# Opening of a two-layer backbone kernel: the first row sums of squares by TensorE, tile by tile, and the first projections by tiles of features

## The chip, the cores and the metric

The kernel runs on one core of one Trainium2 chip, as one program. The metric is the device time of one execution in microseconds (us). Three plain runs of the kernel before took 1098.90, 1098.99 and 1103.02 us, so the time before is their median, 1098.99 us. One more execution was recorded by the hardware profiler; every row below is from that one.

## The reference, cut to what matters

All tensors are float32. There are 1024 latent tokens and 256 context tokens of 1024 features, and two layers. Only the start of layer 0 matters here:

```python
def rms_norm(x, g):
    y = x * lax.rsqrt(jnp.mean(x * x, axis=-1, keepdims=True) + EPS)
    return y * g
def modulate(x, g, shift, scale):
    return rms_norm(x, g) * (1.0 + scale) + shift

shift, scale, gate = split(silu(c) @ ada_w[0] + ada_b[0], 3)
h  = modulate(x, norm_g[0], shift, scale)         # latent tokens
hc = modulate(ctx, norm_g[0], shift_c, scale_c)   # context tokens
kc, vc = split_kv(hc @ w_in[:, K0:G0], k_g)
q, k, v = split_qkv(h @ w_in, q_g, k_g)
...
```

After that come differential attention over 1280 keys, a Fourier mixer, a gated output projection, and a second layer with a short convolution.

## The kernel before, in words

x lies transposed: a tile of x holds 128 features (its partitions) by 512 tokens. There are eight feature tiles (k = 0 to 7) for each half of the tokens, `xs[0]` and `xs[1]`, and eight tiles of 128 features by 256 tokens for the context, `xc`.

The sum of squares of a token therefore runs over the partitions of eight tiles. Before, ScalarE squares each of the eight tiles (lines 196 and 199), VectorE adds the squares up elementwise into two running tiles `ssq` and then adds these two (lines 200 and 202), and TensorE sums over partitions at the end (`token_sums`, line 209): for each block of 128 tokens a product of the 128x128 block of `ssq` as the stationary operand with one column of ones, whose result is one column of `ps_ss`. Four blocks of tokens make four such products for a half of the latents, two for the context.

From `ps_ss` the rows of 1/rms are made by a chain through four engines: VectorE (216), GpSimd's power (218), a diagonal matrix `dg` by VectorE (220), a product of ones with it by TensorE (228, `ps_r`), a copy by ScalarE (234, `r`). Then `x_scale` (387) multiplies a tile of x by its scale and by `r`, `x_hi` (393) adds the shift and rounds to float32r, and `x_lo` (397) keeps the rest. Scale and shift of a feature tile come from `ada_first` (123), `ada_ev` (128), `ada_col` (135) and `ada_use` (144, 147, 150). For the first half, tile k = 0 has its scales from the first call of `ada_first`, k = 1 from the second.

A projection is computed for tiles of 128 tokens by 512 outputs. Six of them, `accs[0]` to `accs[5]`, are open at once in PSUM: four tiles of latents of the first half and then two of context. `proj_step` adds the share of one feature tile to one of them by three products (284 to 286: hi by hi, lo by hi, hi by lo). `steps(j, i...)` does that for the feature tiles 2j and 2j + 1, for each of the named accumulators in turn.

The order on TensorE, VectorE, ScalarE and GpSimd in the opening is that in which the code is written (`manual_schedule`); DMAs are issued by SyncE. An engine works off its queue in order, so an instruction that waits holds back all behind it. The buffers named `sq` come from a pool slot of four, which `ada_ev` shares.

Of the kernel before, what the change touches and what calls it, by code (L numbers as in the profile page):

```python
# [8 lines left out]
F32 = mybir.dt.float32  # L9
F32R = mybir.dt.float32r  # L10
AF = mybir.ActivationFunctionType
# [6 lines left out]
P = 128  # L18
# [4 lines left out]
KT = 8  # L23
# [6 lines left out]
NB = 512  # L30
# [7 lines left out]
def block_kernel(tc, A):  # L38
    nc = tc.nc
# [3 lines left out]
    def opn(name, side="left", space=None):  # L43
        kw = dict(name=name, bufs=1, side=side, reuse_waits="tile")
        if space is not None:
            kw["space"] = space
        cm = tc.tile_pool(**kw)
        pools[name] = (cm, cm.__enter__())
        return pools[name][1]
# [19 lines left out]
    pst = opn("pst", space=PSUM)  # L69
# [9 lines left out]
    ones = const.tile([P, P], F32, name="ones")  # L79
# [6 lines left out]
    xs = [[None] * KT for _ in range(2)]  # L86

    def load_x(half):
# [9 lines left out]
        out=cs[:, :, 0:2], in_=small[:, S_C:S_C + 16].rearrange("p (k r) -> p k r", r=2), func=AF.Silu)  # L98
# [5 lines left out]
        out=bias1, in0=small[:, S_B:S_B + 48].rearrange("p (l k) -> p l k", l=2)[:, :, 8:16],  # L104
# [84 lines left out]
    def squares_sum(tiles, n, pool):  # L189

        a = [pool.tile([P, NB], F32, name="ssq", tag="th", bufs=2) for _ in range(2)]

        def step(k):
            dst = a[k % 2]
            if k < 2:
                nc.scalar.activation(out=dst[:, :n], in_=tiles[k], func=AF.Square)
            else:
                sq = pool.tile([P, NB], F32, name="sq", tag="o", bufs=4)
                nc.scalar.activation(out=sq[:, :n], in_=tiles[k], func=AF.Square)
                nc.vector.tensor_add(out=dst[:, :n], in0=dst[:, :n], in1=sq[:, :n])  # L200
            if k == KT - 1:
                nc.vector.tensor_add(out=a[0][:, :n], in0=a[0][:, :n], in1=a[1][:, :n])
        return step, a[0]

    def token_sums(parts, n):
        ps = pst.tile([P, 8], F32, name="ps_ss", tag="t", bufs=2)
        for i in range(n // P):
            for a in parts:
                nc.tensor.matmul(ps[:, i:i + 1], lhsT=a[:, i * P:(i + 1) * P], rhs=ones[:, 0:1],
                                 start=a is parts[0], stop=a is parts[-1])  # L210
        return ps
# [40 lines left out]
    post = opn("post", "right")  # L252
# [24 lines left out]
    def proj_step(ps, tt, c, k):  # L277
        if tt < NTC:
            hh, hl = (a[:, tt * P:(tt + 1) * P] for a in HC[k])
        else:  # L280
            half, o = divmod(tt - NTC, 4)
            hh, hl = (a[:, o * P:(o + 1) * P] for a in H[half][k])
        whi, wlo = (w[:, (k % 2) * NB:(k % 2 + 1) * NB] for w in W[4 * c + k // 2])
        nc.tensor.matmul(ps, lhsT=hh, rhs=whi, start=k == 0, stop=False)  # L284
        nc.tensor.matmul(ps, lhsT=hl, rhs=whi, start=False, stop=False)  # L285
        nc.tensor.matmul(ps, lhsT=hh, rhs=wlo, start=False, stop=k == KT - 1)  # L286
# [8 lines left out]
    def proj_tok(tt, c, at=()):  # L295
        ps = acc.tile([P, NB], F32, name="ps_tok", tag="acc", bufs=6)
        for k in range(KT):
            if k in at:
                tick()
            if k == 7:  # L300
                tick(cols)
            proj_step(ps, tt, c, k)
        return ps
# [70 lines left out]
    for k in range(KT):  # L374
        t = hcp.tile([P, TC], F32, name="xc", tag="hc", bufs=17)
        nc.sync.dma_start(out=t, in_=A["ctxT"][k])
        xc.append(t)
    first = [2, 3, 4, 5, 0, 1]
    accs = [acc.tile([P, NB], F32, name="ps_tok", tag="acc", bufs=6) for _ in first]
# [41 lines left out]
    def steps(j, *tiles):  # L421
        for i in tiles:
            for k in (2 * j, 2 * j + 1):
                proj_step(accs[i], first[i], 0, k)

    def diag(ps, n):
        return rms_diag(ps, n, post, ("sqk", 1))

    def ada_ps():
        return pst.tile([P, NB], F32, name="ps_ada", tag="t", bufs=2)  # L430
# [12 lines left out]
        gt[w] = (t1, t2)  # L443

    HA, HB = slice(0, NB), slice(NB, 2 * NB)
    sq0, a0 = squares_sum(xs[0], NB, post)
    for k in range(KT):
        sq0(k)
    ps = token_sums([a0], NB)
    psa = ada_ps()  # L450
    ada_first(psa, araw[0])
    d0 = diag(ps, NB)
# [23 lines left out]
    def ada_next():  # L476
        psa = ada_ps()
        a = araw.pop(0)
        ada_half(psa, a, 0)
        ada_half(psa, a, 1)  # L480
        return ada_ev(psa)
# [3 lines left out]
        whalf(raw, w, HA, G)  # L485
        whalf(raw, w, HB, G)

    steps(0, 0, 1)
    psc = token_sums([ac], TC)
    dc = diag(psc, TC)  # L490
    steps(0, 2)
    ev = ada_next()
    w_split()
    araw.append(ada_load(0, 3))
# [104 lines left out]
    for tt in range(NK):  # L599
# [5 lines left out]
        ps = proj_tok(tt, 1, (4,))  # L605
        if tt:
# [4 lines left out]
                          in_=v.rearrange("p (h d) -> p h d", h=NH))  # L611
# [504 lines left out]
    def proj_feat2(w, half, at={}):  # L1116
        ps = acc.tile([P, NB], F32, name="ps_feat", tag="acc", bufs=6)
        for k in range(KT):
            if k in at:
                at[k]()  # L1120
            a, b = (w[k // 4][:, i, (k % 4) * P:(k % 4 + 1) * P] for i in range(2))
            nc.tensor.matmul(ps, lhsT=a, rhs=Y[half][k][0], start=k == 0, stop=False)  # L1122
            nc.tensor.matmul(ps, lhsT=a, rhs=Y[half][k][1], start=False, stop=False)
            nc.tensor.matmul(ps, lhsT=b, rhs=Y[half][k][0], start=False, stop=k == KT - 1)
        return ps
# [304 lines left out]
    for half in range(2):  # L1430
        y0(half)
        for f in range(KT):
# [5 lines left out]
            if pend:  # L1438
                ps = pend.pop(0)
            else:  # L1440
                ps = proj_feat2(W[half * KT + f], half)
# [229 lines left out]
```

## Time and profile before

| what | value |
|---|---|
| runs of the kernel | 1098.90, 1098.99, 1103.02 us |
| profiled execution, its own time | 1103.36 us |
| its span (first to last instruction) | 1101.6 us |
| mean granted TensorE clock | 0.981 |
| TensorE busy | 1037.6 us, 94% of the span |
| VectorE, ScalarE, GpSimd busy | 69%, 44%, 44% |
| DMA traffic | 131.12 MB, mean 119 GB/s |

Times in the rows are microseconds from the start of the span. PE is TensorE's matmuls and PEld its weight loads; a float32 product is recorded as two passes, so four products stand as x8. A row of the timeline gives start, duration, engine, line, operation, output<-inputs, shapes and count, and behind it in brackets the idle time ahead of it with what ended it. A row of the table by stretches gives, for a stretch of the span, its length, the busy time and number of instructions of PE, PEld, DVE, ACT and POOL, then the granted TensorE clock (1.00 is full, 0.50 half), the DMA share and GB/s. Ahead of the first record of the clock, which falls at about 21.9 us, the column reads 1.00 by default.

### The profile page before, as it was taken

Reading aid. Unit: us, or ns where it says so; the run is one execution under the profiler, and the core shown is the slowest. Engines: PE = TensorE matmul, PEld = TensorE weight load, DVE = VectorE, ACT = ScalarE, POOL = GpSimd, SP = SyncE. Lnnn points to the kernel's source line nnn. Section 1 sums busy time; section 2 is a strip of 40 time slices with the busy share of each in tenths; the row PEclk is TensorE's granted clock in tenths of the full one; section 3 lists DMA queues with packets and bytes.
Section 4 is the critical chain, followed back from the end, with each engine's and each line's share of the span. In section 5 each row is a group of like instructions: output and inputs, shape, how many; then the busy total and the mean of one; then the engine's idle time right before and its main releaser. Section 6 shows DMA issues by size and latency. Waiting matters only on the chain.

```text
span 1101.6 us, 14113 instructions
## 1 busy us (share of the span) xinstructions
PE 1037.6 (94%) x5118; PEld 846.6 (77%) x5118; DVE 756.2 (69%) x1079; ACT 481.7 (44%) x876; POOL 484.6 (44%) x412
## 2 busy tenths in 40 slices
PE   3998999999999899999999998899999999999798
PEld 2666888878877689899888886578888888787576
DVE  4599966957886388888853287985636645579842
ACT  4353323312445377777753363633333333353420
POOL 1247115620455047766574445655354353432331
PEclk9999999999999999999999998999999999999899
DMA  9733896353112978161006560121111112212421
GB/s 330 302 124 94 247 378 226 106 153 129 58 43 77 247 178 188 31 167 58 11 21 207 170 194 22 38 77 39 60 55 58 58 39 69 66 57 67 159 95 62
DMA packets 61381, 131.12 MB, mean 119 GB/s; under 512 B 5248, under 2 KB 30208, under 8 KB 58112
## 3 DMA queue, kind: packets, MB, share of 16 engines
q1 hardware_dynamic: 60240, 125.64, 35.9%
q0 software_dynamic: 1072, 4.59, 1.2%
q8 instruction: 40, 0.66, 0.2%
q14 instruction: 29, 0.24, 0.1%
HBM read 105.57 MB, written 24.64 MB: 118 GB/s over the span
## 4 chain that ended last, share of the span: by engine, by line
PE 64%; DVE 20%; POOL 5%; issue 5%; ACT 5%; DMA 0%; ACTq 0%; POOLq 0%; DVEq 0%
PE psX L651 6%; PE psX L653 6%; PE psX L652 6%; PE ps_av L1069 5%; PE ps_tok L284 3%; PE ps_tok L285 3%; PE ps_tok L286 3%; PE psY L652 3%; PE psY L653 3%; PE psY L651 3%; PE S L1019 3%; PE S L1020 3%; DVE nm L1024 2%; PE ps_t L1059 2%; PE ps_feat L1122 2%
## 5 line engine op out<-in xcount | busy, mean ns | idle before, releaser
L61 ACT CAST wop<-wraw 128x512 fp32r<-128x512 f32 x152 | 93.1, 620 | 127.4 <-PE psY L653 30.1
L62 POOL TENSOR_TENSOR wop<-wraw,wop 128x512 fp32r<-128x512 f32 x72 | 100.8, 1403 | 70.4 <-ACT wop L61 68.8
L284 PE MATMUL ps_tok<-whi,hhi 128*128 128x512 f32 x288 | 118.6, 412 | 4.5 <-ACT hhi L393 3.6
L285 PE MATMUL ps_tok<-whi,hlo 128*128 128x512 f32 x288 | 115.2, 400 | 3.8 <-DVE hlo L397 3.8
L286 PE MATMUL ps_tok<-wlo,hhi 128*128 128x512 f32 x288 | 114.3, 397 | 0.0
L1024 DVE TENSOR_REDUCE nm<-S 128x1 f32<-128x1280 f32 x64 | 95.1, 1487 | 22.4 <-PE S L1020 19.4
L651 PE MATMUL psX<-B,wop 128*128 128x512 f32 x240 | 98.2, 409 | 12.0 <-DVE out L1400 3.9
L1035 ACT ACTIVATE p<-S,nm 128x1280 f32<-128x1280 f32 x64 | 85.2, 1331 | 45.0 <-DVE nm L1024 41.2
L652 PE MATMUL psX<-B,wop 128*128 128x512 f32 x240 | 97.4, 406 | 1.6 <-POOL B L1491 1.0
L653 PE MATMUL psX<-B,wop 128*128 128x512 f32 x240 | 97.0, 404 | 0.5 <-POOL wop L62 0.5
L630 POOL TENSOR_TENSOR s<-wraw 128x512 f32<-128x512 f32 x20 | 27.6, 1382 | 125.1 <-DMA wraw<-in_wodd_dram 118.1
L62 DVE TENSOR_TENSOR wop<-wraw,wop 128x512 fp32r<-128x512 f32 x80 | 66.5, 833 | 20.6 <-ACT wop L61 20.3
L1069 PE MATMUL ps_av<-v,aT 128*128 128x128 f32 x640 | 76.8, 275 | 0.0
L630 POOL TENSOR_TENSOR wraw<-wraw 128x512 f32<-128x512 f32 x40 | 56.5, 1420 | 43.2 <-DVE wop L62 35.8
L1069 PEld LDWEIGHTS ps_av<-v,aT 128*128 128x128 f32 x640 | 74.2, 192 | 0.2
L284 PEld LDWEIGHTS ps_tok<-whi,hhi 128*128 128x128 f32 x288 | 55.3, 192 | 18.6 <-ACT hhi L393 4.5
L1046 POOL TENSOR_TENSOR p<-p,cc 128x256 f32<-128x256 f32 x32 | 40.3, 1258 | 65.7 <-DVE cc L1043 46.5
L285 PEld LDWEIGHTS ps_tok<-whi,hlo 128*128 128x128 f32 x288 | 55.2, 192 | 17.9 <-DVE hlo L397 7.1
L651 PEld LDWEIGHTS psX<-B,wop 128*128 128x128 f32 x240 | 46.3, 193 | 27.0 <-issue 5.4
L652 PE MATMUL psY<-B,wop 128*128 128x512 f32 x160 | 63.5, 397 | 2.7 <-DVE B L1253 2.3
L653 PE MATMUL psY<-B,wop 128*128 128x512 f32 x160 | 63.3, 396 | 1.5 <-DVE wop L62 1.5
L286 PEld LDWEIGHTS ps_tok<-wlo,hhi 128*128 128x128 f32 x288 | 55.2, 192 | 12.0 <-DVE wlo L172 0.2
(339 smaller groups left out, 2661.8 us busy)
## 6 DMA issues: line engine op xcount, KB each, us to landing
ada_raw<-in_ada_dram SPq DMA_DIRECT2D x24, 1024.0 KB, 8.0
wraw<-in_wodd_dram SPq DMA_DIRECT2D x32, 512.0 KB, 3.5
wraw<-in_wo_dram SPq DMA_DIRECT2D x24, 512.0 KB, 4.3
wraw<-in_wtok_dram SPq DMA_DIRECT2D x16, 512.0 KB, 5.8
arena<-kd SPq DMA_DIRECT2D x16, 320.0 KB, 8.9
kq<-kd SPq DMA_DIRECT2D x16, 320.0 KB, 9.6
xt<-in_xT_dram SPq DMA_DIRECT2D x16, 256.0 KB, 6.4
xr<-in_xT_dram SPq DMA_DIRECT2D x16, 256.0 KB, 3.9
```

The source lines that it names most:

```text
L61: nc.scalar.copy(out=o[:, 0, :], in_=src)
L62: eng.tensor_tensor(out=o[:, 1, :], in0=src, in1=f32(o[:, 0, :]), op=ALU.subtract)
L284: nc.tensor.matmul(ps, lhsT=hh, rhs=whi, start=k == 0, stop=False)
L285: nc.tensor.matmul(ps, lhsT=hl, rhs=whi, start=False, stop=False)
L286: nc.tensor.matmul(ps, lhsT=hh, rhs=wlo, start=False, stop=k == KT - 1)
L630: tt = lambda out, x, y, op: nc.gpsimd.tensor_tensor(out=out, in0=x, in1=y, op=op)
L651: nc.tensor.matmul(ps, lhsT=a, rhs=x[k][0], start=start and k == 0, stop=False, skip_group_check=not start)
L652: nc.tensor.matmul(ps, lhsT=a, rhs=x[k][1], start=False, stop=False, skip_group_check=not start)
L653: nc.tensor.matmul(ps, lhsT=b, rhs=x[k][0], start=False, stop=k == 3, skip_group_check=not start)
L1024: nc.vector.tensor_reduce(out=nm, in_=S[m][:, :NKEY], op=ALU.max, axis=AX.X, negate=True)
L1035: nc.scalar.activation(out=p, in_=S[m][:, :NKEY], func=AF.Exp, bias=tiles.pop((i, m, "nm")), accum_out=z)
L1069: nc.tensor.matmul(ps, lhsT=groups[i, k // 4][:, (k % 4) * P:(k % 4 + 1) * P], rhs=v[:, k * P:(k + 1) * P], start=k == 0, stop=k == NK - 1)
```

## The change

The squares of the first half of the latents are no longer added up by VectorE. ScalarE squares a feature tile, and TensorE at once sums its four blocks of tokens over partitions and adds the result to `ps_ss` in PSUM: four products for each of eight tiles, in place of four in all. The second half and the context keep the old way. Further down, the first six steps on TensorE are written out with the feature tile as the outer loop (accumulators 0, 1, 2 for k = 0, and then for k = 1), and the sums of the context's squares, which stood between accumulators 1 and 2, stand behind all of them.

```diff
-    sq0, a0 = squares_sum(xs[0], NB, post)
+    ps = pst.tile([P, 8], F32, name="ps_ss", tag="t", bufs=2)
     for k in range(KT):
-        sq0(k)
-    ps = token_sums([a0], NB)
+        sq = post.tile([P, NB], F32, name="sq", tag="o", bufs=4)
+        nc.scalar.activation(out=sq, in_=xs[0][k], func=AF.Square)
+        for i in range(4):
+            nc.tensor.matmul(ps[:, i:i + 1], lhsT=sq[:, i * P:(i + 1) * P], rhs=ones[:, 0:1], start=k + i == 0,
+                             stop=k == KT - 1, skip_group_check=i > 0)
     psa = ada_ps()
     ada_first(psa, araw[0])
     d0 = diag(ps, NB)
...
-    steps(0, 0, 1)
+    for k in range(2):
+        for i in range(3):
+            proj_step(accs[i], first[i], 0, k)
     psc = token_sums([ac], TC)
     dc = diag(psc, TC)
-    steps(0, 2)
     ev = ada_next()
```

On TensorE, the start of the queue (- before, + after; the names are output<-inputs, x4 and x32 count products):

```order
-L1664 UNCONDITIONAL_BRANCH
-L209 MATMUL ps_ss<-ones,ssq 128x1 x4
+L1670 UNCONDITIONAL_BRANCH
+L453 MATMUL ps_ss<-ones,sq 128x1 x32
 L123 MATMUL ps_ada<-ada_raw,cs 32x256 x8
 L228 MATMUL ps_r<-dg,ones 128x512
```

Thirty-two products now stand ahead of `ada_first` and `ps_r`, where four stood.

On TensorE, the first steps of the projections, before (ps_tok_152, 153 and 154 are accumulators 0, 1 and 2; hhi_219 and hlo_220 are the feature tile k = 0, hhi_243 and hlo_244 are k = 1):

```order
L284 MATMUL ps_tok_152<-whi_202,hhi_219 128x512
L285 MATMUL ps_tok_152<-whi_202,hlo_220 128x512
L286 MATMUL ps_tok_152<-wlo_203,hhi_219 128x512
L284 MATMUL ps_tok_152<-whi_202,hhi_243 128x512
L285 MATMUL ps_tok_152<-whi_202,hlo_244 128x512
L286 MATMUL ps_tok_152<-wlo_203,hhi_243 128x512
L284 MATMUL ps_tok_153<-whi_202,hhi_219 128x512
L285 MATMUL ps_tok_153<-whi_202,hlo_220 128x512
L286 MATMUL ps_tok_153<-wlo_203,hhi_219 128x512
```

and after (152, 153 and 154 are the same accumulators; hhi_240 is k = 0, hhi_264 is k = 1):

```order
L284 MATMUL ps_tok_152<-whi_223,hhi_240 128x512
L285 MATMUL ps_tok_152<-whi_223,hlo_241 128x512
L286 MATMUL ps_tok_152<-wlo_224,hhi_240 128x512
L284 MATMUL ps_tok_153<-whi_223,hhi_240 128x512
L285 MATMUL ps_tok_153<-whi_223,hlo_241 128x512
L286 MATMUL ps_tok_153<-wlo_224,hhi_240 128x512
L284 MATMUL ps_tok_154<-whi_223,hhi_240 128x512
L285 MATMUL ps_tok_154<-whi_223,hlo_241 128x512
L286 MATMUL ps_tok_154<-wlo_224,hhi_240 128x512
L284 MATMUL ps_tok_152<-whi_223,hhi_264 128x512
```

Before, three products stand ahead of the first that needs k = 1; after, nine. The context's two sums (line 209, `ps_ss`) come behind twelve products before and behind eighteen after; in both, the next conditioning products (line 117) come behind all eighteen.

On VectorE the seven adds leave the queue:

```order
 L271 COPY gains<-small 128x64
 L265 TENSOR_SCALAR g_102<-small 128x1
-L200 TENSOR_TENSOR ssq<-ssq,sq 128x512 x6
-L202 TENSOR_TENSOR ssq<-ssq 128x512
 L216 TENSOR_SCALAR rs<-ps_ss 128x4
 L220 TENSOR_TENSOR dg<-cst,rs 128x512
```

ScalarE has eight squares of the same size in both. Behind the steps shown, and on GpSimd and SyncE from the first row on, the queues read the same.

## The prediction

> **What bounds the kernel.** I read the page first, then the opening in order of time, then its busy times by stretches, then the same kind of work wherever it occurs later.
>
> ```profile
> span 1101.6 us, 14113 instructions
> ...
> PE 1037.6 (94%) x5118; PEld 846.6 (77%) x5118; DVE 756.2 (69%) x1079; ACT 481.7 (44%) x876; POOL 484.6 (44%) x412
> ```
>
> TensorE is busy for 94% of the span, so a time gained or lost in the opening is gained or lost whole unless something later takes it up. The opening in order of time:
>
> ```profile
> 5.95 0.63 ACT L196 ACTIVATE ssq<-xt 128x512 f32<-128x512 f32 x1 [0.92 <-DMA xt<-in_xT_dram]
> 7.46 0.63 ACT L196 ACTIVATE ssq<-xt 128x512 f32<-128x512 f32 x1 [0.89 <-DMA xt<-in_xT_dram]
> 8.13 2.60 ACT L199 ACTIVATE sq<-xt 128x512 f32<-128x512 f32 x4
> 11.02 1.26 ACT L199 ACTIVATE sq<-xt 128x512 f32<-128x512 f32 x2 [0.30 <-DMA xt<-in_xT_dram]
> 13.05 0.69 DVE L202 TENSOR_TENSOR ssq<-ssq 128x512 f32<-128x512 f32 x1
> 13.79 1.87 PE L209 MATMUL ps_ss<-ones,ssq 128*128 128x1 f32 x8 [13.79 <-DVE ssq L202]
> 15.59 1.93 PE L123 MATMUL ps_ada<-ada_raw,cs 128*32 128x256 f32 x16
> 15.70 0.16 DVE L216 TENSOR_SCALAR rs<-ps_ss 128x4 f32<-128x4 f32 x1 [1.96 <-PE ps_ss L209]
> 17.00 0.69 DVE L220 TENSOR_TENSOR dg<-cst,rs 128x512 f32<-128x512 f32 x1 [1.14 <-POOL rs L218]
> 17.84 2.05 PE L228 MATMUL ps_r<-dg,ones 128*128 128x512 f32 x2 [0.31 <-DVE dg L220]
> 20.56 1.73 PE L123 MATMUL ps_ada<-ada_raw,cs 128*32 128x256 f32 x16
> ...
> 22.90 0.61 PE L135 MATMUL ps_col<-cst,ada_ev 128*128 128x2 f32 x4 [0.61 <-ACT ada_ev L128]
> 23.37 0.47 PE L284 MATMUL ps_tok<-whi,hhi 128*128 128x512 f32 x1
> ```
>
> The reader is to see a single chain: squares arrive until 12.28 (11.02 + 1.26), VectorE's last add ends at 13.74, the eight passes end at 15.66, and from there rs, dg, ps_r and the conditioning products lead to the first projection at 23.37. TensorE has nothing to do ahead of 13.79.
>
> **The passes: a loss of 4.8 us.** What does one of the 1-column passes cost? The same eight, cut finer, and the only ones of a later stage that are at hand:
>
> ```profile
> 14.24 0.99 PE L209 MATMUL ps_ss<-ones,ssq 128*128 128x1 f32 x4
> ...
> 15.31 0.35 PE L209 MATMUL ps_ss<-ones,ssq 128*128 128x1 f32 x1
> ...
> 60.63 0.95 PE L209 MATMUL ps_ss<-ones,ssq 128*128 128x1 f32 x8
> ```
>
> The third pass starts at 14.24, the eighth at 15.31: (15.31 - 14.24) / 5 = 0.214 us from one to the next, and the last takes 0.35. At 60.63 eight take 0.95, 0.119 each: there the clock is full, here it is evidently half. The change issues 32 products, 64 passes. The first can start when the first square is done, 5.95 + 0.63 + 0.05 = 6.63 (0.05 is the step from 13.74 to 13.79). A feature tile needs eight passes, 1.71 us at 0.214, and squares come faster (8.09 for the second, then four in 2.60), so TensorE never waits again. The last pass starts at 6.63 + 63 x 0.214 = 20.11 and ends at 20.46, against 15.66: **4.8 us later**. The seven VectorE adds that leave, 1.46 us of them on the path after the last square, are inside this difference. ScalarE's squares wait for one of four buffers (the eighth for tile 3's passes, at 6.63 + 4 x 1.71 = 13.5), which delays nothing, as ScalarE's next instruction needs ada_first. The first ada_first stands behind the passes and moves by the same 4.8 us, and with it all up to 23.37.
>
> The other end is the full clock from the first pass: eight tiles at 0.95, the second at 8.14, end 8.14 + 7 x 0.95 = 14.79, 0.9 us earlier than before. So the term lies between -0.9 and +4.8. Which clock is it? By stretches of one period of the clock's changes:
>
> ```profile
> 18.50:21.95 3.45, 3.42 (x22) 1.69 (x20) 1.14 (x4) 0.66 (x2) 1.26 (x1) 1.00 0.98 287
> 21.95:25.36 3.41, 1.75 (x15) 0.93 (x7) 2.49 (x5) 1.42 (x3) 1.28 (x1) 1.00 1.00 406
> 25.36:28.78 3.42, 2.44 (x5) 1.66 (x6) 2.46 (x7) 3.17 (x9) 0.00 (x0) 0.50 1.00 423
> 28.78:32.20 3.42, 3.42 (x11) 2.85 (x11) 1.14 (x4) 0.00 (x0) 0.37 (x1) 0.50 0.48 198
> ...
> 59.50:62.92 3.42, 3.13 (x23) 2.81 (x22) 2.26 (x6) 2.42 (x5) 0.84 (x1) 1.00 0.94 355
> 62.92:66.30 3.38, 3.38 (x10) 2.24 (x9) 3.11 (x5) 0.00 (x0) 3.38 (x4) 0.50 0.60 247
> ```
>
> The clock falls after a stretch in which TensorE worked 1.75 of 3.41 us, and comes back after one in which it worked all of 3.42. But it also falls after 59.50 to 62.92, where it was "busy" for 3.13 us: that stretch holds the eight 1-column passes above and eight 2-column ones. They load weights and multiply almost nothing, and the clock counts them as next to nothing. I take +4.8 us: 64 such passes do not raise the clock.
>
> [...]
>
> Passes that are quick from the first one on, the lower end of -0.9, are counted with rival (a).
>
> **The steps: a gain of 2.6 us.**
>
> ```profile
> 26.34 0.80 PE L284 MATMUL ps_tok<-whi,hhi 128*128 128x512 f32 x1 [2.03 <-ACT hhi L393]
> 27.13 0.80 PE L285 MATMUL ps_tok<-whi,hlo 128*128 128x512 f32 x1
> ...
> 29.43 0.63 PE L284 MATMUL ps_tok<-whi,hhi 128*128 128x512 f32 x1
> 29.85 0.63 PE L285 MATMUL ps_tok<-whi,hlo 128*128 128x512 f32 x1
> ...
> 30.71 0.85 PE L209 MATMUL ps_ss<-ones,ssq 128*128 128x1 f32 x4
> ...
> 32.55 0.40 PE L284 MATMUL ps_tok<-whi,hhi 128*128 128x512 f32 x1
> 32.79 0.39 PE L285 MATMUL ps_tok<-whi,hlo 128*128 128x512 f32 x1
> ...
> 33.34 1.92 PE L117 MATMUL ps_ada<-ada_raw,cs 128*32 128x512 f32 x16
> ...
> 29.37 0.42 DVE L202 TENSOR_TENSOR ssq<-ssq 128x256 f32<-128x256 f32 x1
> ```
>
> After three products TensorE waits 2.03 us for the feature tile k = 1, and the clock then falls: products follow each other by 0.42 (29.43, 29.85) and not by 0.24 (32.55, 32.79). In the new order nine products stand ahead of that wait. In times of before: 23.37 + 9 x 0.24 = 25.5; k = 1 at 26.34 as before, its lo part at 27.13, eight more products by 27.13 + 8 x 0.24 = 29.1. The stretch from 21.95 then holds six more products, 1.4 us, 3.1 in all and 2.5 without the four 2-column products, so that the clock stays. The context's sums, moved behind, wait for the squares (29.37 + 0.42 = 29.79), take 0.5 at that clock, and the products of line 117 start at 30.4 instead of 33.34: 2.9 us earlier. If the clock stays at half through all eighteen, they end at 23.37 + 18 x 0.43 = 31.1, the sums at 31.95, line 117 at 32.0: 1.3 us earlier. Between 1.3 and 2.9 I take 2.6, nearer to the end at which TensorE has no idle stretch left that would lower the clock.
>
> ```profile
> 35.33 0.58 ACT L128 COPY ada_ev<-ps_ada 128x512 f32<-128x512 f32 x1 [6.60 <-PE ps_ada L117]
> 36.85 0.37 ACT L234 COPY r<-ps_r 128x256 f32<-128x256 f32 x1
> 38.68 0.50 PE L284 MATMUL ps_tok<-whi,hhi 128*128 128x512 f32 x1 [0.61 <-ACT hhi L393]
> ```
>
> That is passed on: ScalarE waits 6.60 us for line 117, then its splits and the context's r follow, and at 38.68 TensorE waits for what comes of r. The context's sums themselves may move by 1 us at no cost, since `ps_r` of the context stands behind line 117 on TensorE. The loads wait for TensorE, not the reverse:
>
> ```profile
> SPq L111 <- PE ps_ada L117: 17.5, 5, 9.3
> ```
>
> SyncE's queue waits 17.5 us in five waits for line 117 to free a buffer, so the transfers move with it.
>
> **The sum.** +4.8 - 2.6 = +2.2 us. The profiled execution took 1103.36 us (span 1101.6), 4.4 above the median of the runs, 1098.99, and would come to 1105.6; against the median it is 1101.2 us, +0.2%. The runs of before differ by 4 us between themselves, so less than about 0.5%, 5.5 us, can't be told from no change.
>
> **Rivals.**
> (a) The passes count as work, and the clock rises after one period of 3.4 us, between 10.0 and 13.5. Then 16 to 32 passes are slow and the rest take 0.119: the sums end between 15.9 and 17.4, +0.2 to +1.7, in the middle +1.0. Behind them ps_r (2.05) and ada_first (1.73) run at about half that, some 1.9 us less, and the steps gain their full 2.9. Total 1.0 - 1.9 - 2.9 = -3.8: 1095.2 us; with passes at 0.119 from the first on, 1.9 less, 1093.3. For it: TensorE would be in steady use from 6.63. Against it: the stretch 59.50:62.92. [...]
> (b) The clock stays at half right through the steps and on to the fourth accumulator. Line 117 then starts at 32.0 but takes twice 1.92 (+1.9, so that nothing is left of the gain but 1.3 - 1.9 = -0.6), and six products behind it cost 0.19 more each, 1.1. Together +4.8 + 0.6 + 1.1 = +6.5: 1105.5 us, slower by 0.6%. It decides if the clock is still at half 14 us after the first product. Against it: 28.78:32.20, one stretch of steady products that raised it.
> (c) Something later takes the shift up, as VectorE sets the pace at 60 to 80 us, or the steps gain all that the passes lose: 1099.0 us, no change. VectorE's work there follows from the same opening, which speaks against it.
>
> **How the numbers follow.** The forecast 0.60, (a) 0.15, (b) 0.08, (c) 0.17. The range goes from 1096.0, most of (a) out to its upper side, to 1105.0: the forecast's +2.2 on a run as slow as the slowest of before (1103.02) gives 1105.2, and (b) 1105.5. About 0.2 is left out. Faster by over 0.5% needs more than (a) gives, 0.04; slower by over 0.5% is most of (b) and a slow median, 0.11; within 0.5%, 0.85.
>
> **What would show it.** 64 passes of line 453 from 6.6 us with starts 0.214 apart, ending at 20.5; first projection at about 28.2; then nine products, a wait of under 1 us for k = 1, and line 117 at about 35.2 (30.4 + 4.8). Passes 0.11 apart would show (a); products 0.42 apart through to line 117, (b); line 117 at 33 or earlier makes the forecast wrong.

## The result, and the profile after

The changed kernel is slower: 1106.13 us (median of 20 runs, 1101.16 to 1109.43) against 1100.66 us (20 runs of before, 1097.23 to 1103.78). The ratio is 1.0051, with an interval of 1.0039 to 1.0063; that is 5.5 us, between about 4.3 and 6.9. The forecast was +2.2. The two profiled executions alone differ by only 2.0 us (1103.36 and 1105.41), since that of before was itself a long one: 1103.36 against a median of 1100.66. Of the kernels below, passes_only had one execution of 5788 us, which its ratio leaves out.

The page of the changed kernel, its first line and its busy times:

```profile
span 1103.6 us, 14213 instructions
...
PE 1047.6 (95%) x5174; PEld 857.5 (78%) x5174; DVE 752.2 (68%) x1072; ACT 481.7 (44%) x876; POOL 484.3 (44%) x412
```

TensorE has 56 passes more (5174 for 5118) and is busy 10 us longer, VectorE 4 us less. The opening of the changed kernel in order of time (start, duration, engine, line):

```profile
5.16 0.63 ACT L451 ACTIVATE sq<-xt 128x512 f32<-128x512 f32 x1
5.84 1.87 PE L453 MATMUL ps_ss<-ones,sq 128*128 128x1 f32 x8 [5.84 <-ACT sq L451]
7.48 3.41 ACT L451 ACTIVATE sq<-xt 128x512 f32<-128x512 f32 x5 [1.69 <-DMA xt<-in_xT_dram]
8.16 12.11 PE L453 MATMUL ps_ss<-ones,sq 128*128 128x1 f32 x56 [0.45 <-ACT sq L451]
11.82 0.63 ACT L451 ACTIVATE sq<-xt 128x512 f32<-128x512 f32 x1 [0.93 <-PE ps_ss L453]
13.53 0.63 ACT L451 ACTIVATE sq<-xt 128x512 f32<-128x512 f32 x1 [1.08 <-PE ps_ss L453]
20.20 1.93 PE L123 MATMUL ps_ada<-ada_raw,cs 128*32 128x256 f32 x16
20.30 0.16 DVE L216 TENSOR_SCALAR rs<-ps_ss 128x4 f32<-128x4 f32 x1 [16.37 <-PE ps_ss L453]
22.44 1.82 PE L228 MATMUL ps_r<-dg,ones 128*128 128x512 f32 x2 [0.31 <-DVE dg L220]
...
27.57 0.77 PE L284 MATMUL ps_tok<-whi,hhi 128*128 128x512 f32 x1
28.15 0.63 PE L285 MATMUL ps_tok<-whi,hlo 128*128 128x512 f32 x1
...
30.28 0.60 PE L284 MATMUL ps_tok<-whi,hhi 128*128 128x512 f32 x1
30.71 0.41 PE L285 MATMUL ps_tok<-whi,hlo 128*128 128x512 f32 x1
...
34.02 0.58 PE L209 MATMUL ps_ss<-ones,ssq 128*128 128x1 f32 x4 [0.61 <-DVE ssq L202]
34.52 1.92 PE L117 MATMUL ps_ada<-ada_raw,cs 128*32 128x512 f32 x16
```

The reader is to see the forecast's opening. Fifty-six passes take 12.11 us, 0.21 each, and end at 20.27; `rs` starts at 20.30 where it started at 15.70. The first projection stands at 27.57 (23.37 before), and line 117 at 34.52 (33.34 before). Nowhere among the first nine products does TensorE wait for the feature tile k = 1. The first seven run at half clock: 28.15 to 30.71 for six of them, 0.43 us each.

The clock by its periods in the changed kernel (columns as in the prediction: PE, PEld, DVE, ACT, POOL, granted clock, DMA share, GB/s):

```profile
23.91:27.32 3.41, 2.10 (x24) 1.17 (x23) 1.76 (x5) 1.96 (x4) 0.57 (x1) 1.00 0.80 292
27.32:30.73 3.41, 3.41 (x11) 2.73 (x11) 2.25 (x6) 1.22 (x4) 1.27 (x1) 0.50 0.84 290
30.73:34.15 3.42, 2.81 (x14) 2.04 (x12) 2.94 (x8) 2.08 (x7) 0.00 (x0) 1.00 0.47 193
```

It is full for one period ahead of the first projection, falls after 2.10 busy us of 3.41, and comes back after a full one. So the opening costs what was forecast, and the rest of the 5.5 us must lie behind it.

### The profile page after: what moved, and what is told of

It reads as the page before. It is cut to its first block, busy times and chain, and to the rows that moved or that the text cites. A ratio compares the mean times of both kernels' runs of the same rounds, so it can differ in the third digit from the quotient of the medians.

```text
span 1103.6 us, 14213 instructions
## 1 busy us (share of the span) xinstructions
PE 1047.6 (95%) x5174; PEld 857.5 (78%) x5174; DVE 752.2 (68%) x1072; ACT 481.7 (44%) x876; POOL 484.3 (44%) x412
## 4 chain that ended last, share of the span: by engine, by line
PE 64%; DVE 21%; issue 5%; POOL 5%; ACT 4%; DMA 1%; ACTq 0%; POOLq 0%; DVEq 0%
PE psX L657 6%; PE psX L659 6%; PE psX L658 6%; PE ps_av L1075 5%; PE ps_tok L285 3%; PE ps_tok L284 3%; PE ps_tok L286 3%; PE psY L659 3%; PE psY L658 3%; PE psY L657 3%; PE S L1025 3%; PE S L1026 2%; DVE nm L1030 2%; PE ps_t L1065 2%; PE ps_feat L1128 2%
```

## The experiments

All kernels below are compared with the kernel before on the same chip. "Opening" is the start of the first copy of line 351 (`th<-ps_t`), at about 100 us, against the mean of three profiles of before, 99.6. "Behind the opening" is what the timed ratio, times 1099 us, leaves when the opening's part is taken off; the intervals of the ratios make it uncertain by 1.3 to 2.7 us. The theory that the expectations put first is that the loss behind the opening arises where the conditioning weights are loaded and comes with the opening's lag; the rivals are the clock, chance, and the number of instructions. The openings are of one profile each, except before and the change, and differ by up to 0.9 us between profiles of the same kernel; that comes on top.

**The two halves of the change.** One kernel has the passes and the old order of steps, one the new order and VectorE's adds.

```diff
 passes_only: after, with
-    for k in range(2):
-        for i in range(3):
-            proj_step(accs[i], first[i], 0, k)
-    psc = token_sums([ac], TC)
+    steps(0, 0, 1)
+    psc = token_sums([ac], TC)
 ...
+    steps(0, 2)
 steps_only: before, with the reverse edit
```

> The first half of the change alone: 64 one-column passes on TensorE in place of VectorE's adds; the steps of the projections stay in their old order. Theory 1 (the prediction's sum was right in each term for the profiled pair, but the steps gain less in an ordinary execution than in the profiled one of before, whose clock fell to half between 25.4 and 32.2 us): passes 0.214 us apart, sums ready 4.6 to 4.8 us later than before, time +4.8 us, ratio about 1.0044. Theory 2 (the passes themselves cost more than 4.8 us, something behind them loses as well): +6 us or more, ratio 1.0055 or more.

> The second half of the change alone: the order of the first six steps, with VectorE's adds kept. Theory 1: where the clock does not fall in the old order, that order ends its eighteen products only some 1.4 us later than the new one, so the time is between -1.4 and 0 us, ratio about 0.999. The prediction's term: -2.6 us, ratio 0.9976. Theory 2 needs nothing of this one; -2.6 us would speak for it.

passes_only: ratio 1.0075 (1.0052 to 1.0098), 8.2 us; its sums end at 20.25, its opening is 4.7 us late. steps_only: 0.9994 (0.9979 to 1.0008), -0.7 us; its line 117 starts at 30.55 and its opening is 1.35 us early. So the passes cost 4.7 us in the opening, as forecast, and about 3.5 more (uncertain by 2.5) behind it. The steps alone gain 1.35 us in the opening, half of the forecast's 2.6; beside the passes they gain 2.7 (the opening is at 104.33 in passes_only and at 101.66 in the mean of the change's profiles).

**Do more passes lift the clock?** Each of the 32 products is issued twice, the second time into four unused columns.

```diff
+        for i in range(4, 8):
+            nc.tensor.matmul(ps[:, i:i + 1], lhsT=sq[:, (i - 4) * P:(i - 3) * P], rhs=ones[:, 0:1], start=False,
+                             stop=k == KT - 1, skip_group_check=True)
```

> The change with each of its 32 one-column products issued a second time, into four further columns that nobody reads: 128 passes. If a pass costs 0.214 us at half clock throughout: 64 x 0.214 = 13.7 us more than the change, some +19 us against before, ratio about 1.0175. If a long row of such passes lifts the clock, the later ones are 0.11 apart, and it is +7 us over the change or less, ratio about 1.011.

1.0180 (1.0155 to 1.0204). The passes of the doubled kernel, grouped by line, and the last of them:

```profile
L453 PE MATMUL ps_ss<-ones,sq 128*128 128x1 f32 x64 | 14.8, 352 | 6.1 <-ACT sq L451 6.1
L456 PE MATMUL ps_ss<-ones,sq 128*128 128x1 f32 x64 | 14.8, 352 | 0.0
```

```profile
31.68 1.84 PE L456 MATMUL ps_ss<-ones,sq 128*128 128x1 f32 x8
33.46 1.93 PE L123 MATMUL ps_ada<-ada_raw,cs 128*32 128x256 f32 x16
35.70 1.93 PE L228 MATMUL ps_r<-dg,ones 128*128 128x512 f32 x2 [0.31 <-DVE dg L220]
```

128 passes run without a gap from 6.06 to 33.5. Each is recorded as 352 ns long, but they overlap and start 0.21 us apart, and the last eight still take 1.84 us together, where eight took 0.95 at the full clock (in before, at 60.63). The first record of the clock comes only at 37.4 us; by this pace it stays at half through 27 us of passes. Rival (a), which had it rise between 10.0 and 13.5 us, is out.

**The reverse: the old opening with a full clock.** Useless products ahead of the sums (14 of ones, and one of 256 columns with each tile of x), with VectorE's adds kept:

```diff
+    for n in range(14):
+        nc.tensor.matmul(accs[5][:, 0:P], lhsT=ones, rhs=ones, start=True, stop=True)
     for k in range(KT):
         sq0(k)
+        nc.tensor.matmul(accs[5][:, 0:2 * P], lhsT=ones, rhs=xs[0][k][:, 0:2 * P], start=True, stop=True)
```

> The kernel before, with products that nobody reads put where TensorE is idle, ahead of 13.8 us (fourteen 128x128 by 128 products of ones, then one of ones with 256 columns of each tile of x as it arrives), so that the clock is full when the sums of squares are ready. Theory 1: passes, ps_r and the conditioning products run at full clock, 0.9 + 0.85 + 0.3 + 0.8 us less on the way to the first projection, -2 to -3 us, ratio 0.9975. If the clock of the opening does not matter: 1.000.

0.9992 (0.9974 to 1.0009). The first rows of that kernel's TensorE:

```profile
6.88 5.02 PE L451 MATMUL ps_tok<-xt,ones 128*128 128x256 f32 x16
13.38 1.05 PE L209 MATMUL ps_ss<-ones,ssq 128*128 128x1 f32 x8 [1.48 <-DVE ssq L202]
14.36 1.07 PE L123 MATMUL ps_ada<-ada_raw,cs 128*32 128x256 f32 x16
```

Behind these wider products the eight passes take 1.05 us where they took 1.87, near the 0.95 of the full clock: by that pace the clock has risen. The opening is 1.15 us early; the times do not show it beyond their interval.

**How far single executions differ.** Two more profiles each of before and after, unedited.

> The kernel before, unchanged, profiled once more. The question is whether its first profile is a typical execution: it took 1103.36 us where the median of its plain runs is about 1100. Theory 1: half clock falls on other places of the opening in this execution; where it spares the stretch from the first projections to 33 us, the products of line 117 start at 31 to 32 us instead of 33.34, and the first copy of a transposed tile (line 351) at 96.5 to 98.5 instead of 99.98. Theory 2 (something behind the opening loses with the new passes): the opening of this profile is as long as the first one's, 100 us to that copy.

> The same as before_b, for one more phase of the clock's periods. Theory 1: the start of line 117 and of line 351 spread over 1 to 3 us between the profiles and go with the number of half-clock periods in the first 100 us. Theory 2: they don't move.

> The changed kernel, unchanged, profiled once more. The passes end at 20.2 us in every execution, since 64 of them never lift the clock. Theory 1: line 117 at 34.5 to 36.5 us (up to 2 us later than in its first profile, 34.52, if the clock stays at half through the steps), line 351 at 102 to 104. Theory 2: line 117 at 34.5 as before, and more time behind 100 us than the 1001.6 us of the first profile.

> The same as both_b, for one more phase. Theory 1: on average over the profiles of both kernels, the changed one reaches line 351 some 5 us later than the kernel before, with what comes behind equal within 1 us. Theory 2: less than 4 us there, the rest behind.

Before took 1096.01 and 1095.50 us, the changed kernel 1102.37 and 1104.27. With three profiles of each, the opening is at 99.98, 99.23 and 99.58 us before, and at 102.05, 101.82 and 101.11 after: 2.06 us in the mean. From there to the end there are 1001.6, 995.0 and 994.2 us before, and 1001.6, 998.8 and 1001.4 after. The difference behind the opening, 3.7 us in the mean, is of the size that the times ask for, but single executions of before differ by twice as much. That goes with the clock: behind the opening its records have 9.9, 5.2 and 4.3 periods of 3.4 us at half clock before, and 8.9, 7.3 and 8.9 after. At about 1.4 us each, which is what the profiles of before differ by, some 2.6 of these 3.7 us are the clock's in these six executions. The plain runs have no such difference: the mean granted clock is 0.9856 in the 20 runs of the changed kernel and 0.9856 in the 23 of before that stand beside passes_only, and in both, by a straight line through the runs, one that was granted 0.01 less is some 4.3 us longer.

Where is it? One place shows in the rows. Between 140 and 230 us the next conditioning weights, 1 MB at a time, are loaded beside the stores of keys and values. ScalarE and TensorE there, in before_c, where the load is in time (the brackets hold the wait):

```profile
159.05 2.56 ACT L574 ACTIVATE ada_raw<-ada_raw,cs 128x512 f32<-128x512 f32 x4 [2.18 <-DVE ada_sum L577]
```

and in both_c:

```profile
163.53 2.56 ACT L580 ACTIVATE ada_raw<-ada_raw,cs 128x512 f32<-128x512 f32 x4 [5.14 <-DMA ada_raw<-in_ada_dram]
```

A later load and the split of a weight tile behind it, in before_c and then in both_c, and what TensorE meets in both_c:

```profile
209.76 2.57 ACT L574 ACTIVATE ada_raw<-ada_raw,cs 128x512 f32<-128x512 f32 x4 [1.35 <-DMA ada_raw<-in_ada_dram]
212.72 1.98 ACT L171 CAST whi<-wraw 128x1024 fp32r<-128x1024 f32 x2
```

```profile
214.55 2.56 ACT L580 ACTIVATE ada_raw<-ada_raw,cs 128x512 f32<-128x512 f32 x4 [4.60 <-DMA ada_raw<-in_ada_dram]
217.50 1.99 ACT L171 CAST whi<-wraw 128x1024 fp32r<-128x1024 f32 x2
```

```profile
222.96 0.51 PE L286 MATMUL ps_tok<-wlo,hhi 128*128 128x512 f32 x1 [1.40 <-DVE wlo L172]
```

The transfers of that stretch, from issue to landing, of before_c and of both_c:

```profile
ada_raw<-in_ada_dram SPq DMA_DIRECT2D x9, 1024.0 KB, 8.1
```

```profile
ada_raw<-in_ada_dram SPq DMA_DIRECT2D x9, 1024.0 KB, 9.2
```

A load lands late and ScalarE waits 5.14 us for it; at 214.55 it waits again, 4.60 us where it waited 1.35, so that its split of a weight tile starts 4.8 us later, and at 222.96 TensorE waits 1.40 us for VectorE's `wlo`, for which it does not wait in before_c. TensorE then does less between 215 and 235 us, by stretches, first before_c and then both_c:

```profile
215.00:225.00 10.00, 10.00 (x52) 8.32 (x51) 9.06 (x12) 1.89 (x3) 8.40 (x7) 1.00 0.54 143
225.00:235.00 10.00, 7.80 (x37) 6.22 (x36) 6.76 (x12) 2.60 (x4) 0.90 (x1) 1.00 0.42 121
```

```profile
215.00:225.00 10.00, 8.60 (x41) 6.33 (x39) 9.78 (x12) 5.56 (x9) 8.54 (x7) 1.00 0.25 61
225.00:235.00 10.00, 7.45 (x36) 5.78 (x36) 9.03 (x17) 3.65 (x5) 4.90 (x4) 0.97 0.61 181
```

It is busy 1.75 us less in these 20 us, and its clock falls there for a part of them (0.97 granted). The products of the two kernels, laid side by side in queue order, are 1.53 us apart at 213 us, which is what their openings differ by, and 5.81 us at 235. In all 18 profiles with the full loads (those below included) the two waits come together: in ten of them ScalarE waits 4.33 to 5.93 us for that load and TensorE 0.83 to 1.40 us for `wlo`; in the other eight ScalarE waits 2.18 to 3.46 us and TensorE not for `wlo`. Laid beside the mean of the three profiles of before, product by product, TensorE is up to 213 us where its opening put it in all 18, within 0.4 us. By 225 us the ten have fallen back by 1.7 to 2.9 us more, and the eight by between -0.2 and 0.9. Of the four profiles in which the opening is that of before and nothing is added to TensorE (before, before_b, before_c and before_pad below), none shows it; of the change's four, three do (after, both_c and both_pad, but not both_b).

**With half of these loads.** Four of the eight later conditioning blocks are left out, in before and in after; half of the second layer's shifts and scales, and its gates, are then constants.

```diff
-    adas = [(0, 4), (0, 5)] + [(1, j) for j in range(6)]
+    adas = [(0, 4), (0, 5)] + [(1, j) for j in range(2)]
```

> The kernel before with four of the eight later blocks of conditioning left out (half of layer 1's scales and shifts and its gates are constants), so that the loads between 125 and 205 us, which fill the DMA engines, are half as many. It is the base for both_light: only the difference of the two counts. By itself somewhat quicker than the kernel before, as VectorE and ScalarE have less to do there: -2 to -10 us.

> The changed kernel with the same blocks left out. Theory 1 (the opening loses some 2 us in the profiles, and the rest of the measured 5.5 us is lost where conditioning loads and stores fill the DMA engines, at 150 to 235 us, and by half-clock periods): against before_light +2 to +3 us. Theory 2 (the opening loses 5 us in an ordinary execution): against before_light +5 to +6 us.

0.9946 (0.9934 to 0.9958) and 0.9969 (0.9955 to 0.9983): 2.5 us apart by the ratios, 3.2 by the medians (1092.90 and 1096.08), each uncertain by about 2. The openings are 2.4 apart (100.39 and 102.80). Neither profile has a wait of TensorE for `wlo` there. With the loads thinned, the change costs what its opening costs, within that uncertainty, which still leaves room for up to 2 us behind it.

**The lag without the passes.** Seven useless squares on ScalarE ahead of the eighth one delay the sums.

```diff
+        if k == KT - 1:
+            for _ in range(7):
+                nc.scalar.activation(out=accs[5], in_=xs[0][0], func=AF.Square)
```

> The kernel before with seven squares that nobody reads ahead of ScalarE's eighth square, 0.63 us each, so that the sums of squares come about 4.4 us later with no pass added and no order changed. Theory A (being late in the opening is the whole cost, whatever comes behind): the same as the passes alone, +4.4 us in the opening and 1.0075 in all, about +8 us. Theory B (the passes do something more, by their number of instructions or by where their tiles lie): +4.4 us in all, ratio 1.004.

1.0045 (1.0032 to 1.0059), 4.9 us. Its `rs` starts at 19.06, its opening is 3.3 us late, 1.6 us are left behind it, and its profile has no wait for `wlo`. A lag alone is passed on, with 1.6 us more, which is about what the times and the one opening leave uncertain.

**The instructions without the lag, and passes without a lag.** count_only is before with 28 useless one-column products in idle time; pairs lets VectorE add the squares of two tiles, so that 32 passes remain.

```diff
 count_only:
+    for n in range(28):
+        nc.tensor.matmul(accs[5][:, n:n + 1], lhsT=ones, rhs=ones[:, 0:1], start=True, stop=True)
 pairs (in after's loop, two tiles at a time):
+        nc.vector.tensor_add(out=pr[0], in0=pr[0], in1=pr[1])
```

> The kernel before with 28 useless 1-column products of ones ahead of the opening's squares, that is with as many TensorE instructions as the changed kernel, but in time in which TensorE has nothing to do (56 passes at 0.21 us are 12 us, from about 1 to 13.8). The sums should end where they do before, within 0.5 us. Theory 1 (the excess behind the opening comes with the lag, as what runs beside the conditioning loads is moved against them): no change, a ratio within 0.9985 to 1.0015. Rival (the excess comes with the number of TensorE instructions, which moves the places at which instructions are fetched among the conditioning loads): the sums' end unmoved, but about +2.5 us behind 140 us, a ratio of about 1.002 to 1.003.

> The change with VectorE adding the squares of two feature tiles, so that 16 products, 32 passes, are issued instead of 64. The last pair's sum comes at about 13.7 us and its eight passes end at about 15.6, as before the change; the steps keep their order. Opening: 1.3 to 1.8 us ahead of before. Theory 1 (loss follows lag): a ratio of 0.998 to 0.9995. Rival (loss follows the number of TensorE instructions, 12 more here): 1.000 to 1.001.

count_only: 1.0005 (0.9993 to 1.0017), with `rs` at 15.86. The number of instructions costs nothing that can be measured. Its one profile has the late load all the same (TensorE waits 1.39 us at 221.66). pairs: 1.0012 (0.9998 to 1.0027), although its `rs` starts at 15.94 and its opening is 1.9 us early; 3.2 us are missing behind it. So the loss does not follow the lag, here with an uncertainty of about 2 us, and r_pad below repeats it.

**Single passes.** Squares and ones in float32r: 32 products of two columns, one pass each, of which the first column is used.

```diff
+    ones_r = const.tile([P, 2], F32R, name="ones_r")
+    nc.scalar.copy(out=ones_r, in_=ones[:, 0:2])
-            nc.tensor.matmul(ps[:, i:i + 1], lhsT=sq[:, i * P:(i + 1) * P], rhs=ones[:, 0:1], ...
+            nc.tensor.matmul(ps[:, 2 * i:2 * i + 2], lhsT=sq[:, i * P:(i + 1) * P], rhs=ones_r, ...
-    d0 = diag(ps, NB)
+    d0 = diag(ps.rearrange("p (i r) -> p i r", r=2)[:, :, 0], NB)
```

r_passes lacks the last edit and takes the row sums from columns 0 to 3, that is those of the first two blocks of tokens, each twice; r_fixed has it.

> The changed kernel with squares and ones rounded to float32r, so that a product is one pass and not two: 32 passes. At half clock 0.214 us each, eight tiles at 0.86 us, TensorE follows the squares and ends some 1 us after the last of them, at 13.5 us against 15.66: -2.2 us, and the steps -1.4 us: -3.6 us against before, ratio 0.9967. If a float32r pass takes twice as long, the sums end at 20.2 and nothing is gained over the change, 1.005.

> The change with squares and ones in float32r: 32 products of two columns, each a single pass, of which the first column is used. The rounding of the squares is that of this type. Sums end at about 14.2 to 14.5 us, 1.3 us ahead of before, and the steps keep their gain of about 1.5: opening 2.5 to 3 us ahead of before. If nothing is lost behind the opening where it comes earlier: 1097 against 1100, a ratio of 0.9965 to 0.998. Rival (the quicker pace of products that showed between 580 and 1000 us with these instructions, 0.2266 us and not 0.2333, belongs to where the program's instructions lie and not to its data): 0.987 to 0.989.

r_passes 0.9879 (0.9864 to 0.9893), r_fixed 0.9896 (0.9872 to 0.9920): 11 us faster than before. The opening of r_fixed explains a part:

```profile
6.68 7.05 PE L455 MATMUL ps_ss<-ones_r,sq 128*128 128x2 f32 x32 [6.68 <-ACT sq L453]
13.74 1.93 PE L123 MATMUL ps_ada<-ada_raw,cs 128*32 128x256 f32 x16
```

The sums end at 13.7 instead of 15.7, and the opening is 3.3 us early. The other 8 us come from products of the later layers that follow each other faster all along (from 780 to 820 us r_fixed has 178 of them, before_b 173).

**Where the buffers lie.** The tile `ones_r` takes 32 bytes of the pool of constants, so that what is placed behind it (`hhi`, `hlo`, `whi`, `wlo`, `gop`, `wop`) begins at 32 past a multiple of 64 bytes, and not at a multiple. Three kernels tell the place from the type: before and after with a useless tile of the same size, and r_fixed with one more, which brings the buffers back to multiples of 64.

```diff
+    pad = const.tile([P, 2], F32, name="pad")
+    nc.scalar.copy(out=pad, in_=ones[:, 0:2])
```

> The kernel before with a useless tile of 8 bytes a partition, copied once by ScalarE, in the place of the pool in which r_fixed keeps its ones in float32r: it takes 32 bytes, and each buffer placed behind it (hhi, hlo, whi, wlo, gop, wop among them) begins 32 bytes later, at 32 past a multiple of 64 instead of at a multiple. If the quicker pace of r_fixed comes from where its buffers lie: products with gop and wop follow each other at 0.226 us and not at 0.234, 8 us less in all, a ratio of 0.992 to 0.994. Rival (it comes from the float32r squares): 0.999 to 1.001.

> The changed kernel with the same 32 bytes. If the buffers' place sets the pace: 8 us less than the changed kernel (1.005), a ratio of 0.996 to 0.999 to the kernel before as it was, and about 1.003 to 1.006 to before_pad. Rival: 1.004 to 1.006.

> r_fixed with 32 bytes more, so that all buffers behind begin at multiples of 64 again. If the place sets the pace: products at 0.234 us, and only the opening's gain of 2.5 to 3 us stays, 0.9965 to 0.999. Rival (float32r squares): 0.989 as r_fixed.

before_pad 0.9910 (0.9894 to 0.9925), both_pad 0.9966 (0.9952 to 0.9981), r_pad 1.0003 (0.9988 to 1.0017). Products one after the other, of before_b, before_pad, r_fixed and r_pad:

```profile
791.23 0.40 PE L652 MATMUL psX<-B,wop 128*128 128x512 f32 x1
791.46 0.39 PE L653 MATMUL psX<-B,wop 128*128 128x512 f32 x1
791.69 0.40 PE L651 MATMUL psX<-B,wop 128*128 128x512 f32 x1
```

```profile
791.20 0.39 PE L654 MATMUL psX<-B,wop 128*128 128x512 f32 x1
791.43 0.39 PE L655 MATMUL psX<-B,wop 128*128 128x512 f32 x1
791.65 0.39 PE L653 MATMUL psX<-B,wop 128*128 128x512 f32 x1
```

```profile
791.23 0.39 PE L659 MATMUL psX<-arena,wop 128*128 128x512 f32 x1
791.46 0.39 PE L660 MATMUL psX<-arena,wop 128*128 128x512 f32 x1
791.68 0.39 PE L661 MATMUL psX<-arena,wop 128*128 128x512 f32 x1
```

```profile
791.16 0.40 PE L662 MATMUL psX<-arena,wop 128*128 128x512 f32 x1
791.39 0.40 PE L663 MATMUL psX<-arena,wop 128*128 128x512 f32 x1
791.63 0.40 PE L661 MATMUL psX<-arena,wop 128*128 128x512 f32 x1
```

Over two steps the rows show 0.46, 0.45, 0.45 and 0.47 us; over 40 us they are plain. The stretch from 780 on in before_b, before_pad and r_pad:

```profile
780.00:820.00 40.00, 40.00 (x173) 32.12 (x172) 22.61 (x36) 15.05 (x25) 16.46 (x12) 1.00 0.16 53
```

```profile
780.00:820.00 40.00, 40.00 (x179) 33.10 (x178) 23.20 (x37) 14.86 (x26) 18.20 (x13) 1.00 0.16 53
```

```profile
780.00:820.00 40.00, 40.00 (x173) 32.22 (x172) 21.52 (x36) 14.32 (x24) 17.70 (x13) 1.00 0.16 53
```

At the same full clock 179 products are done instead of 173 in 40 us: 0.2235 and 0.2312 us by these counts, which take in the products that the ends of the stretch cut, and 0.227 and 0.234 as the median from one product to the next. It is the place and not the type. The places that the built kernels give their tiles, laid beside the traces, tell more than this: the pace goes with whether the two operands of a product begin alike. These are the steps from one float32r product of 512 columns to the next at full clock, by where the operands begin (bytes past a multiple of 64), in before and, in the last row, in before_pad:

| moving operand | stationary operand | steps | for example | median, us |
|---|---|---|---|---|
| 0 | 0 | 899 | latents, moving `whi` and stationary `hhi`, `hlo` | 0.227 |
| 0 | 32 | 96 | context, moving `whi` and stationary `hhi`, `hlo` | 0.2325 |
| 32 | 0 | 2050 | moving `B`, stationary `wop` | 0.234 |
| 32 | 32 | 3055 | latents, context and `wop` alike | 0.227 |

Products of `S` (`S<-kq`, `S<-arena`) are not in the table: both operands come from one tile there, and they step by 0.232 to 0.233 in either kernel. r_pad, back at multiples of 64, has the slow products again and an opening 4.0 us early, of which the times show nothing: about 4 us are missing behind it.

The last pair also repeats the main comparison with buffers elsewhere: both_pad is 1.0057 times before_pad (0.9966 / 0.9910; with the two intervals about 1.0036 to 1.0078), 6.2 us, of which the openings hold 2.3.

## Why the prediction was wrong

**The passes: right.** 64 passes 0.21 apart, a start at 5.84 instead of 6.63 with a wait for the second tile's square behind the first eight, an end at 20.27 against 20.46 forecast. Their term was +4.8; `rs` measured +4.6 and the opening of passes_only +4.7.

**The clock: right.** 128 passes do not lift it (the last eight of double take 1.84 us), let alone 64. Rival (a), at 0.15, did not come true; the rows of one stretch (59.50:62.92) had it right.

**The steps: right in size, by luck in part, and not in the reason.** The forecast took -2.6 between -1.3 and -2.9; beside the passes they gave -2.7, alone -1.35, each uncertain by some 0.9. No idle time for k = 1 is left, where the forecast had a wait of under 1 us. But the clock was at half through the first seven products all the same, after a period that holds only 2.10 busy us of 3.41 (the forecast counted on 2.5 to 3.1); it came back after one full period, so that rival (b) did not come true. Line 117, forecast at about 35.2, starts at 34.52, 35.15 and 33.67 in the three profiles.

**The sum of the opening: right.** +2.2 forecast, +2.06 measured in three profiles each.

**The step that failed** is "That is passed on ... so the transfers move with it": everything behind line 117 was taken to move by the opening's 2.2 us, and no rival had a price behind it. Rival (c) let something later take the shift up; nothing in the prediction let something later add to it. The runs show 3.4 us more (5.5 - 2.06). What fails is not that a lag passes on: up to 213 us it does in all 18 profiles, within 0.4 us. But where the squares are summed on TensorE, 3.2 to 4.3 us are missing behind the opening in six of eight kernels, whether it is late or early. The other two, r_fixed and r_passes, are compared with before_pad across chips, and are uncertain by 3.1 and 2.3 us:

| kernel | ratio x 1099, us | opening, us | behind, us |
|---|---|---|---|
| after | +5.6 | +2.1 | +3.5 |
| passes_only | +8.2 | +4.7 | +3.5 |
| double | +19.8 | +15.9 | +3.9 |
| pairs | +1.3 | -1.9 | +3.2 |
| r_pad | +0.3 | -4.0 | +4.3 |
| both_pad to before_pad | +6.2 | +2.3 | +3.9 |
| r_fixed to before_pad | -1.5 | -3.1 | +1.6 |
| r_passes to before_pad | -3.4 | -2.7 | -0.7 |
| shift_only | +4.9 | +3.3 | +1.6 |
| steps_only | -0.7 | -1.35 | +0.7 |
| before_warm | -0.9 | -1.15 | +0.3 |
| count_only | +0.5 | -0.1 | +0.6 |

A part of it is seen at its place, the late load at 160 us and the wait at 220, worth 1.7 to 2.9 us. It came in three of the change's four profiles, and in none of the three of before and the one of before_pad: this is where the shift was not passed on as it was. They occur in seven of the ten profiles of the kernels in the upper part (down to r_passes, with both_b and both_c), and in three of the eight of the lower part and of before and before_pad. Eight and ten profiles cannot show that this is more than chance, and count_only has the late load in its profile without a loss in its times; so it is no full account.

**What stays open** is what brings this loss on. Against the lag speak pairs and r_pad, whose openings are early and which lose all the same, and less firmly shift_only; against the number of instructions speaks count_only (0.6 us, uncertain by 1.3). What the upper kernels share and the lower ones lack, besides the sums on TensorE, is that the squares' buffers, and with them `dg`, `r` and `ada_ev`, lie at other places of their pool, mostly 4 KB or more away, and so do tiles of later stages that share the pool (`th`, `tl`, `vo`, from which queries, keys and values are stored beside the loads). No kernel moved these alone, so this is a guess. A half clock later on is not it: behind the opening the clock's records have 7.5 such periods in the mean of those eight profiles and 7.9 in the mean of those ten, and the plain runs of before and of the changed kernel were granted the same clock, 0.9856.

The range (1096.0 to 1105.0) missed by 1.1 us. It stood on the median of three runs, 1098.99, where that of twenty is 1100.66, so on the base it assumed the measured 5.5 us would have come to 1104.5, just inside; that would have been luck, since no term behind the opening stood in it. The upper end came from rival (b) and from the spread of before, not from anything behind 40 us; 0.85 for "within 0.5%" was far too sure for a kernel in which 94% of the span is one engine's queue fed by DMAs.

## What to carry to other kernels

A one-column product is no way to fill an idle TensorE: each costs two passes of 0.21 us at half clock for float32, one of 0.22 in float32r (there with two columns), and neither lifts the clock for what follows: the sixteen passes of line 123 take 1.93 us behind either, in after and in r_fixed, and 1.07 behind the wider products of before_warm. A sum over the opening says what the opening does; where a stretch like that from 130 to 180 us follows, in which the DMA engines are busy for 0.99 of the time in before, the time has to be taken on the whole kernel, over several profiles, before a difference of 2 us is believed. And before tuning what lies around the products, look where their two operands begin: 32 bytes were worth 9.9 us here (before_pad), more than the 5.5 us of the whole change, and before_pad and r_fixed beat both kernels.

## What the runs showed of the hardware that was not expected

In the traces of before and before_pad, float32r products of 512 columns whose moving and stationary operands begin alike, both at a multiple of 64 bytes or both at 32 past one, follow each other at 0.227 us; where one begins at a multiple and the other at 32 past it, at 0.2325 to 0.234, at the same full clock. Within before alone both occur. About 2150 steps of before are of the unlike kind, so that 6 ns each would be some 13 us, an estimate; by the times of before_pad (0.9910) it is 9.9. It is not the stationary operand by itself: that of the latents' projections begins at a multiple in before and at 32 past one in before_pad, with 0.227 in both. Why the products of `S` do not follow this was not tried, nor any place but 0 and 32.

27 us of one-column float32 passes without a gap, each with a weight load of 128x128, left the clock at half in double, by their pace (1.87 us for the first eight, 1.84 for the last), where in before_warm 28 passes of 128 columns and 16 of 256, over some 11 us, brought the eight passes of line 209 down from 1.87 to 1.05 us.
